# Attention of a decoder layer: projections five tiles ahead instead of four, the last tile's projection spread over two steps, and one chunk of weights split per step

## The chip, the cores and the metric

The kernel runs on one core of a Trainium2 chip. The metric is the device time of one execution in microseconds (us), as the median of several runs. The core has five engines that run their own instruction queues and wait for each other by semaphores: TensorE (PE, matrix products; its weight loads are shown as PEld), VectorE (DVE), ScalarE (ACT), GpSimd (POOL) and SyncE (SP, which issues transfers).

## The reference

One layer: differential attention over 1024 tokens and 8 heads, then a mixture of experts with 16 experts. Cut to what matters:

```python
def diff_attention(x, w_in, q_gain, k_gain, ..., subln, w_out, lambda_init):
    q, k, v = jnp.split(x @ w_in, [2 * H * dh, 4 * H * dh], axis=-1)
    q = rmsnorm(q.reshape(B, T, H, 2, dh), q_gain) * (dh ** -0.5)
    k = rmsnorm(k.reshape(B, T, H, 2, dh), k_gain)
    v = v.reshape(B, T, H, 2 * dh)
    for s in range(0, T, QBLOCK):                      # QBLOCK = 128
        e = s + QBLOCK
        sc = jnp.einsum('bqhcd,bkhcd->bhcqk', q[:, s:e], k[:, :e])
        sc = jnp.where(dist >= 0, sc - slopes * dist, -jnp.inf)
        p = jax.nn.softmax(sc, axis=-1)
        pd = p[:, :, 0] - lam * p[:, :, 1]
        outs.append(jnp.einsum('bhqk,bkhe->bqhe', pd, v[:, :e]))
    o = rmsnorm(jnp.concatenate(outs, axis=1), subln) * (1.0 - lambda_init)
    return o.reshape(B, T, H * 2 * dh) @ w_out
...
x = x + diff_attention(rmsnorm(x, norm_mix), ...)
x = x + hier_moe(rmsnorm(x, norm_ffn), ...)            # top 2 of 4 experts in the chosen group
```

## The kernel before

Attention is one loop over **steps** g. Head h and tile t of 128 queries belong to step g = 8h + t, so there are 64 of them, 0 to 63. In step g the kernel makes the scores of (h, t) and their softmax, the product with the values of step g - 1 (`pv`), and the **projection** (`qkv`) of a later tile, q = g + LEAD with LEAD = 4. The loop begins at g = -LEAD, so that LEAD projections stand ahead of the first scores. From step E0 = 60 on, where no projections are left, `out_proj` takes their place. Steps are written out in one fixed order; each engine takes its instructions in that order. The mixture of experts follows.

**A projection** has two parts of 12 products each (128 by 384). Each of the eight **chunks** c of the head's weights (128 rows) gives three: high half of x with `wH`, high half of x with `wL`, low half of x with `wH`. Part 0 takes chunks 0 to 3, part 1 chunks 4 to 7. `split_w(h, c)` makes wH on ACT (L243) and then wL on DVE (L244) from the raw chunk `wraw`, which `load_w` fetched. After part 1, ACT copies the values and the queries and keys out of PSUM (`vHL`, `qk`), squares them (`sqk`), and DVE makes the low half of the values (vHL, L323) and the sums `ssq`.

**A pair** of tiles is normalised by `qk_norm` on POOL: 14 small instructions on ssq and then the product `qn` (L339, one buffer). `qk_transpose` turns qn on PE two steps later, at the start of an odd step, and ACT and DVE write the split keys and queries (KM, AH, AL).

**Within a step** PE does: scores; in odd steps the transposes of qn; projection part 0; transposes of the previous step's softmax (`pd_transpose`); projection part 1; pv. On ACT and DVE the splits of weight chunks stand behind the softmax of the step: on DVE the order is bias and maximum (L401), KM, AL, L401 again, pdL (L426), the combination of the two softmaxes (`combine`, L410 to L412), the splits (L244), and then what follows part 1. `o_norm` (POOL, L459 to L465) scales the outputs `ou` of a finished head, and `o_transpose` (PE, L473) turns them: in step 4 of the next head, for head 6 in step 2 of head 7. In the first head each step up to the one of q = 5 also transposes the tile q + 2 of x (L274).

The order of a step around the projection:

```python
        if e >= 0:
            on1(out_proj, e, 0)
        on(qkv, q, 0)
        if t == 2 and h == H - 1:
            o_transpose(h - 1)
        on(pd_transpose, g - 1)
        on(expo, g, 1)
        on(combine, g)
        ...                    # split_w of this step
        on(qkv, q, 1)
        on(pv, g - 1)
```

Of the kernel before, what the change touches and what calls it, by code (L numbers as in the profile page):

```python
# [7 lines left out]
F32 = mybir.dt.float32  # L8
F32R = mybir.dt.float32r
BF = mybir.dt.bfloat16  # L10
# [9 lines left out]
H = 8  # L20
NT = T // 128
# [12 lines left out]
def trunk_layer_kernel(ctx, tc, a, out):  # L34
# [7 lines left out]
    def f(ap):  # L42
        return ap.bitcast(F32)
# [49 lines left out]
    def w_tile(shape, dt, name):  # L93
        return wp.tile(shape, dt, name=name, tag="w")
# [118 lines left out]
    att = es_att.enter_context(tc.tile_pool(name="att", bufs=1))  # L213
# [21 lines left out]
    def split_w(h, c):  # L235

        j = c // 3
        if c % 3 == 0:
            W["H", h, j] = w_tile([128, 3, 384], F32R, "wH")
            W["L", h, j] = w_tile([128, 3, 384], F32R, "wL")  # L240
        wh, wl, r = W["H", h, j][:, c % 3], W["L", h, j][:, c % 3], W["r", h, j][:, c % 3]
        g = gm[:, c:c + 1]
        act.activation(wh, r, AF.Copy, scale=g)  # L243
        vec.scalar_tensor_tensor(wl, r, g, f(wh), op0=OP.mult, op1=OP.subtract)  # L244
# [49 lines left out]
            other = slice(64 * (1 - c), 64 * (2 - c))  # L294
            vec.tensor_scalar(al[other, c], ident[other, None, :].to_broadcast([64, 2, 128]), 0.0, None, op0=OP.mult)
    QK, SS = {}, {}
    LEAD = 4

    def qkv(h, t, part):
        if part == 0:  # L300
            if h == 0 and t < LEAD and t % 2:
                qkv.ps = psQ.tile([128, 384], F32, name="qkv", tag="po", bufs=1)
            elif (8 * h + t >= LEAD and (t - LEAD) % NT in (0, 2)):
                qkv.ps = psS.tile([128, 384], F32, name="qkv", tag="sc")
            else:
                qkv.ps = psQ.tile([128, 384], F32, name="qkv", tag="qkv", bufs=1)
        ps = qkv.ps
        for c in range(4 * part, 4 * part + 4):
            for x, w in ((0, "H"), (0, "L"), (1, "H")):
                pe.matmul(ps, lhsT=hT[t][:, x, c], rhs=W[w, h, c // 3][:, c % 3],  # L310
                          start=(c == 0 and x == 0 and w == "H"), stop=(c == 7 and x == 1))
        if part == 1:
            rs = RX[t]
            if t % 2 == 0:
                QK[h, t // 2] = att.tile([128, 2, 4, 64], F32, name="qk", bufs=2)
                SS[h, t // 2] = att.tile([128, 2, 4], F32, name="ssq", bufs=2)
            qk = QK[h, t // 2][:, t % 2]
            v = att.tile([128, 2, 128], F32R, name="vHL", bufs=13)
            vb = att.tile([128, 128], BF, name="vb", bufs=13)
            VV[h, t] = v, vb  # L320
            act.activation(v[:, 0], ps[:, 256:], AF.Copy, scale=rs)
            act.activation(qk.rearrange("p a b -> p (a b)"), ps[:, :256], AF.Copy, scale=rs)
            vec.scalar_tensor_tensor(v[:, 1], ps[:, 256:], rs, f(v[:, 0]), op0=OP.mult, op1=OP.subtract)  # L323
            sq = att.tile([128, 4, 64], F32, name="sqk")
            act.activation(sq.rearrange("p a b -> p (a b)"), qk.rearrange("p a b -> p (a b)"), AF.Square)
            vec.tensor_reduce(SS[h, t // 2][:, t % 2], sq, axis=AX.X, op=OP.add)  # L326
            act.activation(vb, f(v[:, 0]), AF.Copy)
# [139 lines left out]
    def o_transpose(h):  # L467
        ou, sso = OU.pop(h)
        oT = att.tile([128, T], F32, name="oT")
        for g in range(2):  # L470
            ps = psQ.tile([128, 4, 128], F32, name="tp", bufs=2)
            for k in range(4):
                pe.transpose(ps[:, k], ou[g][:, k], ident)  # L473
            act.activation(oT[:, 512 * g:512 * g + 512], ps.rearrange("p a b -> p (a b)"), AF.Copy,
                           scale=sub08)
        ON[h] = oT
        if h < H - 2:
            sp.dma_start(o_dram[h], oT)
# [11 lines left out]
    def load_wout(k):  # L490

        wo["r", k] = w_tile([128, 2, 512], F32, "woraw")
        c, d = 2 * (k % 4), 512 * (k // 4)
        sp.dma_start(wo["r", k], w_out[:, c:c + 2, d:d + 512])

    def split_wout(k):
        wo[k] = big_tile([128, 2, 2, 512], F32R, "wo", k < 2)
        r = wo.pop(("r", k))
        act.activation(wo[k][:, 0], r, AF.Copy)
        (pool if k == NK - 1 else vec).tensor_sub(wo[k][:, 1], r, f(wo[k][:, 0]))  # L500
# [9 lines left out]
    def prep_o(t):  # L510
        oh = w_tile([128, H, 128], F32R, "oH")
        r = ORAW.pop(t)
        ol = w_tile([128, H, 128], F32R, "oL")
        for dst, src in ((slice(0, H - 2), r), (slice(H - 2, H - 1), ON[H - 2][:, None, t * 128:(t + 1) * 128])):
            act.activation(oh[:, dst], src, AF.Copy)
            vec.tensor_sub(ol[:, dst], src, f(oh[:, dst]))
        ot[t] = oh, ol
# [106 lines left out]
    def route(t):  # L624
        if t >= 0:
            logits(t)
            route_b(t)
        flush()
# [112 lines left out]
    def on(f_, g, *args):  # L741
        if 0 <= g < NT * H:
            f_(g // NT, g % NT, *args)

    def on1(f_, t, *args):
        if 0 <= t < NT:
            f_(t, *args)

    E0, LATE = NT * H - LEAD, 5
    def more_tokens(q):
        if q + 2 < NT:
            transpose_x(q + 2)
            for tiles in {1: [(4, 5)], 3: [(6, 7)]}.get(q, ()):
                norm_x(tiles, pool)
            if q + 5 < NT:
                load_x(q + 5)

    def crossings(g, h, t):  # L760
        if g % 2 and 0 <= g + 1 < NT * H:
            qk_transpose((g + 1) // NT, (g + 1) % NT // 2)
        if t == 4 and 0 < h < H - 1:
            o_transpose(h - 1)

    for g in range(-LEAD, E0 + LATE):
        h, t = divmod(g, NT)
        q = g + LEAD
        e = g - E0
        if t == 0 and 0 <= h < H:  # L770
            vec.tensor_scalar(bias, bias, 0.5, None, op0=OP.mult)
        on(scores, g)
        on(biased, g, 0)
        if g > 2:
            crossings(g, h, t)
        on(expo, g, 0)
        on(biased, g, 1)
        if e >= 0:
            on1(out_proj, e, 0)
        on(qkv, q, 0)  # L780
        if t == 2 and h == H - 1:
            o_transpose(h - 1)
        on(pd_transpose, g - 1)
        on(expo, g, 1)
        on(combine, g)
        if 0 <= h < H - 1:
            if h == 0:
                chunks = {0: (0, 1), 1: (2,), 2: (3, 4), 3: (5, 6, 7)}.get(t, ())
            else:
                chunks = {0: (3,), 1: (4,), 2: (5,), 3: (6, 7)}.get(t, ())  # L790
            for c in chunks:
                split_w(h + 1, c)
        if t >= 5 and 0 <= h < H - 2:
            split_w(h + 2, t - 5)
        if 0 < e + NT < NT - 1:
            c = e + NT - 1
            split_wout(c)
            if c + 4 < NK:
                load_wout(c + 4)
        if e == -1:  # L800
            prep_o(0)
        if e >= 0:
            on1(route_x, e - 1)
            on1(route_i, e - 3)
            on1(route_r, e - 2)
            on1(prep_o, e + 1)
            on1(load_o, e + 2)
            on1(load_res, e + 1)
            on1(out_proj, e, 1)
            on1(o_transpose1, e + 1)  # L810
            route(e - 1)
            on1(residual, e)
        if q == 0:
            transpose_x(1)
            norm_x((2, 3), pool)
        if g <= 2:
            crossings(g, h, t)
        on(qkv, q, 1)
        on(pv, g - 1)
        if q == 0:  # L820
            more_tokens(q)
        if q % 2 and q < NT * H:
            qk_norm(q // NT, q % NT // 2)
        if t == (1 if h < H - 1 else 0) and 0 < h < H:
            o_norm(h - 1)
        if q > 0:
            more_tokens(q)
        if g == -LEAD:
            load_params()
        if g == -LEAD + 1:  # L830
            lambda_and_gains()
            load_w(1)
        if e == -2:
            load_o(0)
        if g == 9:
            routing_constants()
        if t == 3 and 0 <= h < H - 2:
            load_w(h + 2)
        if g == E0 - NT - 1:
            load_gain()  # L840
            for c in range(4):
                load_wout(c)
        if e == -1:
            for c in (NK - 2, NK - 1):
                split_wout(c)
            o_transpose1(0)
            load_o(1)
            load_res(0)
        on1(o_norm1, g - 1 - NT * (H - 1))
# [478 lines left out]
```

## Time and profile before

| | us |
|---|---|
| median of 3 runs (1008.15 to 1012.52) | 1009.61 |
| the profiled execution: its own time | 1010.72 |
| its span, first to last instruction | 1009.0 |
| busy: PE / DVE / ACT / POOL | 940.2 / 814.7 / 753.4 / 329.5 |
| attention's steps, first scores to the end of step 59 | 33.5 to 486.1 |

The profile is one execution on the chip. Busy time is the time in which an engine had an instruction running. Idle time of an engine is written beside the instruction that ended it, with the one that it had waited for. PEclk is the share of TensorE's full clock (2.4 GHz) that was granted.

### The profile page before, as it was taken

How to read it: one execution, taken by the hardware profiler on the slowest of the kernel's cores; microseconds unless marked ns; L12 is line 12 of the kernel's file. 1: busy time of each engine (PE TensorE's matmuls, PEld its weight loads, DVE VectorE, ACT ScalarE, POOL GpSimd, SP SyncE). 2: the span in 40 equal slices, each digit the busy share in tenths (PEclk: the TensorE clock that was granted, in tenths of full speed). 3: DMA queues.
4: the chain of work that ended last, by engine and by line, in shares of the span. 5: the costliest groups of instructions: out<-in, count | busy, mean ns of one | idle time of the engine just before them, and what ended most of it. 6: DMA issues, size and time to landing. Idle time of an engine off the chain costs nothing. (4 is left out here: it accounts for less than half of the span.)

```text
span 1009.0 us, 19952 instructions
## 1 busy us (share of the span) xinstructions
PE 940.2 (93%) x7241; PEld 872.0 (86%) x7241; DVE 814.7 (81%) x1719; ACT 753.4 (75%) x1577; POOL 329.5 (33%) x977
## 2 busy tenths in 40 slices
PE   8989999999999999998899998999999999999992
PEld 7889898998988989888788886789999999999981
DVE  5788887887878888788777777999989899789880
ACT  6877777777787887877653316499899999899971
POOL 3522623325153343516764531301122212121011
PEclk9999999999999999999999999899999999999996
DMA  6320110202011020311233367789999999999923
GB/s 214 85 67 1 49 37 1 85 2 84 1 43 42 2 84 1 125 44 58 59 135 116 119 248 294 269 304 326 342 353 336 336 360 336 342 337 329 331 62 53
DMA packets 75770, 161.72 MB, mean 160 GB/s; under 512 B 8712, under 2 KB 39440, under 8 KB 67472
## 3 DMA queue, kind: packets, MB, share of 16 engines
q1 hardware_dynamic: 70544, 141.87, 39.4%
q0 software_dynamic: 5120, 18.50, 7.8%
q8 instruction: 59, 0.97, 0.4%
q14 instruction: 47, 0.39, 0.1%
HBM read 139.05 MB, written 21.30 MB: 159 GB/s over the span
## 5 line engine op out<-in xcount | busy, mean ns | idle before, releaser
L310 PE MATMUL qkv<-wH,hT 128*128 128x384 f32 x1024 | 291.3, 346 | 7.5 <-DVE vHL L323 6.2
L1005 DVE TENSOR_TENSOR mL<-raw,mH 128x2048 bf16<-128x2048 f32 x95 | 215.6, 2282 | 3.7 <-ACT mH L996 3.6
L310 PEld LDWEIGHTS qkv<-wH,hT 128*128 128x128 f32 x1024 | 188.1, 189 | 11.5 <-DVE vHL L323 9.7
L996 ACT ACTIVATE mH<-raw 128x2048 fp32r<-128x2048 f32 x95 | 177.9, 1904 | 1.2 <-POOL rs_x L56 1.2
L310 PE MATMUL qkv<-wL,hT 128*128 128x384 f32 x512 | 172.2, 336 | 0.4 <-DVE wL L244 0.4
L1071 PE MATMUL gu<-xT,mH 128*128 128x280 f32 x1024 | 156.9, 301 | 2.8 <-DVE xT L1060 1.5
L1071 PEld LDWEIGHTS gu<-xT,mH 128*128 128x128 f32 x1024 | 137.4, 190 | 3.3 <-DVE xT L1060 1.7
L1202 POOL DMA_INDIRECT out_dram<-yo,sidx x20 | 32.4, 1621 | 280.6 <-ACT yo L1200 248.5
L405 ACT ACTIVATE st<-st,nm 128x256 f32<-128x256 f32 (+7 forms) x128 | 99.2, 775 | 15.5 <-DVE nm L401 14.2
L1077 PEld LDWEIGHTS <-mL 128*128 128x128 bf16 x1536 | 93.8, 98 | 10.7
L310 PEld LDWEIGHTS qkv<-wL,hT 128*128 128x128 f32 x512 | 96.9, 189 | 0.7 <-DVE wL L244 0.7
L401 DVE CUSTOM_DVE_ANT_0 st<-sc,bias 128x256 f32<-128x256 f32 (+7 forms) x128 | 93.6, 751 | 2.2 <-PE sc L393 0.2
L426 DVE TENSOR_TENSOR pdL<-tp,pdH 128x512 bf16<-128x512 f32 (+2 forms) x96 | 50.6, 555 | 45.2 <-ACT pdH L425 45.2
L1071 PE MATMUL gu<-hx,mH 128*128 128x280 f32 x512 | 82.3, 303 | 2.4 <-DVE yT L1098 1.8
L450 ACT ACTIVATE sqo<-ou 128x128 f32<-128x128 f32 x64 | 19.9, 311 | 84.9 <-DVE ou L448 84.9
L551 PE MATMUL op<-wo,oH 128*128 128x512 f32 x256 | 81.7, 400 | 1.0 <-DVE vHL L323 0.5
L334 POOL TENSOR_SCALAR ssq<-ssq 128x8 f32<-128x8 f32 x32 | 6.3, 198 | 231.0 <-DVE ssq L326 230.9
L1077 PE MATMUL gu<-xb,mL 128*128 128x140 bf16 x1024 | 80.6, 225 | 0.0
L1071 PEld LDWEIGHTS gu<-hx,mH 128*128 128x128 f32 x512 | 68.9, 189 | 4.3 <-DVE yT L1098 3.3
L392 PE MATMUL sc<-KM,AH 128*128 128x384 f32 (+4 forms) x192 | 64.8, 344 | 0.0
L393 PE MATMUL sc<-KM,AL 128*128 128x384 f32 (+4 forms) x192 | 64.3, 341 | 0.0
L412 DVE SCALAR_TENSOR_TENSOR st<-st,sm,st 128x128 f32<-128x128 f32 (+3 forms) x64 | 61.4, 960 | 2.3
(238 smaller groups left out, 1986.1 us busy)
## 6 DMA issues: line engine op xcount, KB each, us to landing
raw<-in_moe_w_gate_dram SPq DMA_DIRECT2D x32, 1024.0 KB, 7.6
raw<-in_moe_w_up_dram SPq DMA_DIRECT2D x32, 1024.0 KB, 6.5
raw<-in_moe_w_down_dram SPq DMA_DIRECT2D x31, 1024.0 KB, 8.6
wraw<-in_da_w_in_dram SPq DMA_DIRECT2D x64, 192.0 KB, 3.3
out_dram<-xres SPq DMA_DIRECT2D x9, 512.0 KB, 5.2
xraw<-in_x_dram SPq DMA_DIRECT2D x8, 512.0 KB, 6.5
woraw<-in_da_w_out_dram SPq DMA_DIRECT2D x8, 512.0 KB, 3.8
xres<-in_x_dram SPq DMA_DIRECT2D x8, 512.0 KB, 4.3
```

Source lines behind the costliest of these rows:

```text
L310: pe.matmul(ps, lhsT=hT[t][:, x, c], rhs=W[w, h, c // 3][:, c % 3], start=(c == 0 and x == 0 and w == "H"), stop=(c == 7 and x == 1))
L392: pe.matmul(ps[:, k, :wc], lhsT=AH[h, t][:, c], rhs=KM[h][:, c, ks], start=True, stop=False)
L393: pe.matmul(ps[:, k, :wc], lhsT=AL[h, t][:, c], rhs=KM[h][:, c, ks], start=False, stop=True)
L401: vec.tensor_tensor_reduce(sv, tiles[c][:, :n, :wc], bv, -1.0, 3e38, OP.add, OP.min, nm[:, c:c + 1])
L405: act.activation(st[c][:, :w], st[c][:, :w], AF.Exp, scale=-1.0, bias=nm[:, c:c + 1], accum_out=sm[:, c:c + 1])
L412: vec.scalar_tensor_tensor(st[0][:, :w], st[1][:, :w], sm[:, 3:4], st[0][:, :w], op0=OP.mult, op1=OP.add)
L426: vec.tensor_sub(pl[:, g:g + n], ps[:, :n], f(ph[:, g:g + n]))
L551: pe.matmul(ps, lhsT=o[:, c], rhs=wo[4 * half + c // 2][:, w, c % 2], start=(c == 0 and o is oh and w == 0), stop=(c == NK - 1 and o is ol))
L996: act.activation(WH[g], full[g], AF.Copy)
L1005: vec.tensor_sub(WL[g], full[g], f(WH[g]))
L1071: pe.matmul(res[i // 2][:, i % 2, :2 * CAP], lhsT=wh[:, c - c0, 128 * i:128 * i + 128], rhs=rhs[:, c].rearrange("p a b -> p (a b)"), start ...
L1077: pe.matmul(res[i // 2][:, i % 2, :CAP], lhsT=wl[:, c - c0, 128 * i:128 * i + 128], rhs=rb[:, c], start=False, stop=(last and (c0 == 0 or ...
```

## The change

Projections run five tiles ahead (LEAD = 5), so five stand ahead of the first scores. The output projection still begins in step 60. So that the two do not leave a step empty, the projection of the last tile (63) is cut in two: part 0 in step 58, part 1 in step 59. The weights of the next head are needed a step earlier: its first projection stands in step 3 of a head instead of step 4. Chunks are split one per step (0 to 3 in steps 4 to 7 two heads ahead, 4 to 7 in steps 0 to 3 of the head before), where step 3 had two and step 4 none; `load_w` goes from step 3 to step 2. A pair's qk_norm falls into even steps; buffers of qk, ssq, vHL and vb grow by one.

```diff
-    LEAD = 4
+    LEAD = 5
...
-            elif (8 * h + t >= LEAD and (t - LEAD) % NT in (0, 2)):
+            elif 8 * h + t >= LEAD and (t - LEAD) % NT in (0, 2) and h * NT + t < NT * H - 1:
...
-                QK[h, t // 2] = att.tile([128, 2, 4, 64], F32, name="qk", bufs=2)
-                SS[h, t // 2] = att.tile([128, 2, 4], F32, name="ssq", bufs=2)
+                QK[h, t // 2] = att.tile([128, 2, 4, 64], F32, name="qk", bufs=3)
+                SS[h, t // 2] = att.tile([128, 2, 4], F32, name="ssq", bufs=3)
...
-    E0, LATE = NT * H - LEAD, 5
+    E0, LATE = NT * H - 4, 5
...
+    projections = {g: ((g + LEAD, 0), (g + LEAD, 1)) for g in range(-LEAD, E0 - 2)}
+    projections[E0 - 2] = ((NT * H - 1, 0),)
+    projections[E0 - 1] = ((NT * H - 1, 1),)
...
-        on(qkv, q, 0)
+        parts = projections.get(g, ())
+        for q, part in parts[:1]:
+            on(qkv, q, part)
...
-                chunks = {0: (0, 1), 1: (2,), 2: (3, 4), 3: (5, 6, 7)}.get(t, ())
+                chunks = {0: (0, 1), 1: (2, 3, 4), 2: (5, 6), 3: (7,)}.get(t, ())
             else:
-                chunks = {0: (3,), 1: (4,), 2: (5,), 3: (6, 7)}.get(t, ())
+                chunks = {0: (4,), 1: (5,), 2: (6,), 3: (7,)}.get(t, ())
             for c in chunks:
                 split_w(h + 1, c)
-        if t >= 5 and 0 <= h < H - 2:
-            split_w(h + 2, t - 5)
+        if t >= 4 and 0 <= h < H - 2:
+            split_w(h + 2, t - 4)
...
-        on(qkv, q, 1)
+        for q, part in parts[1:]:
+            on(qkv, q, part)
         on(pv, g - 1)
...
-        if q % 2 and q < NT * H:
+        if (NT * H - 1, 0) in parts:
+            pass
+        elif q % 2 and q < NT * H and parts:
             qk_norm(q // NT, q % NT // 2)
...
-        if t == 3 and 0 <= h < H - 2:
+        if t == 2 and 0 <= h < H - 2:
             load_w(h + 2)
```

PE in step 3 of head 2, the end of the projection's part 1 (chunks 6 and 7), with the semaphores that an instruction waits for. Before:

```order
L310 MATMUL qkv<-wH,hT 128x384 x2
L310 MATMUL qkv<-wL,hT 128x384
L310 MATMUL qkv<-wH,hT 128x384 x2
L310 MATMUL qkv<-wL,hT 128x384
L310 MATMUL qkv<-wH,hT 128x384
L437 MATMUL po<-vHL,pdH 128x256 [waits DVE_49]
```

And now:

```order
L310 MATMUL qkv<-wH,hT 128x384 [waits Activation_49]
L310 MATMUL qkv<-wL,hT 128x384
L310 MATMUL qkv<-wH,hT 128x384
L310 MATMUL qkv<-wH,hT 128x384 [waits Activation_49]
L310 MATMUL qkv<-wL,hT 128x384 [waits DVE_49]
L310 MATMUL qkv<-wH,hT 128x384
L437 MATMUL po<-vHL,pdH 128x256 [waits PE_49]
```

The products of this part are now those of the next head's first tile, and the last three wait for the wH (ACT) and the wL (DVE) of chunk 7. DVE in the same step, from the softmax's low half on, before:

```order
L426 TENSOR_TENSOR pdL<-tp,pdH 128x384
L410 RECIPROCAL sm<-sm 128x1
L411 SCALAR_TENSOR_TENSOR sm<-sm,nlam 128x1
L412 SCALAR_TENSOR_TENSOR st_2485<-st_2486,sm,st_2485 128x512
L244 SCALAR_TENSOR_TENSOR wL<-wraw_1778,gm,wH 128x384 x2
L323 SCALAR_TENSOR_TENSOR vHL<-qkv,rs_x_558,vHL 128x128
```

And now:

```order
L426 TENSOR_TENSOR pdL<-tp,pdH 128x384
L410 RECIPROCAL sm<-sm 128x1
L411 SCALAR_TENSOR_TENSOR sm<-sm,nlam 128x1
L412 SCALAR_TENSOR_TENSOR st_2551<-st_2552,sm,st_2551 128x512
L244 SCALAR_TENSOR_TENSOR wL<-wraw_1726,gm,wH 128x384
L323 SCALAR_TENSOR_TENSOR vHL<-qkv,rs_x_198,vHL 128x128
```

One of two splits has left the step; the one that stays, chunk 7, stands behind the combination of step 3. POOL at the start of head 7, where head 6 is normalised (epso, rs_o, ou are o_norm's), before:

```order
L57 TENSOR_SCALAR rs_o<-rs_o 128x8
L58 TENSOR_TENSOR rs_o<-rs_o 128x8
L465 TENSOR_TENSOR ou<-ou,rs_o 128x512 x2
L334 TENSOR_SCALAR ssq<-ssq 128x8
L52 TENSOR_SCALAR rs_qk<-ssq 128x8
L54 TENSOR_TENSOR rs_qk<-rs_qk 128x8
```

And now:

```order
L57 TENSOR_SCALAR rs_qk<-rs_qk 128x8
L58 TENSOR_TENSOR rs_qk<-rs_qk 128x8
L339 TENSOR_TENSOR qn<-qk,rs_qk 128x512
L459 TENSOR_TENSOR epso<-sm 128x8
L460 TENSOR_SCALAR epso<-epso 128x8
L461 TENSOR_SCALAR epso<-sso 128x8
```

The pair that was normalised behind o_norm (its ssq at L334 follows ou) now stands ahead of it: o_norm of head 6 begins behind one more qk_norm.

## Rows read from the trace of the kernel before

**Rows 1.** Stretches: us, busy time of each engine (instructions), granted clock, DMA.

```profile
20.00:30.00 10.00, 10.00 (x65) 9.65 (x63) 6.30 (x18) 7.84 (x20) 6.62 (x30) 1.00 0.45 124
155.40:215.00 59.60, 56.82 (x374) 53.67 (x374) 48.52 (x118) 46.67 (x128) 22.27 (x79) 1.00 0.12 37
```

**Rows 2.** Waits of PE in head 2, 155.4 to 215: us, times, longest.

```profile
PE tp L352 <- POOL qn L339: 1.3, 2, 0.7
PE tp L424 <- DVE AL L369: 0.7, 2, 0.5
PE qkv L310 <- DVE vHL L323: 0.7, 1, 0.7
```

**Rows 3.** Timeline of PE, steps 3 and 4 of head 2: start, us, instruction.

```profile
180.58 0.33 PE L310 MATMUL qkv<-wL,hT 128*128 128x384 f32 x1
...
181.73 0.31 PE L392 MATMUL sc<-KM,AH 128*128 128x320 f32 x1
```

**Rows 4.** Timeline of ACT, step 3 of head 2.

```profile
175.96 0.31 ACT L450 ACTIVATE sqo<-ou 128x128 f32<-128x128 f32 x1 [0.69 <-DVE ou L448]
...
180.99 1.11 ACT L243 ACTIVATE wH<-wraw,gm 128x384 fp32r<-128x384 f32 x2
```

**Rows 5.** Timeline of DVE, step 3 of head 0 and of head 2.

```profile
62.36 0.75 DVE L412 SCALAR_TENSOR_TENSOR st<-st,sm,st 128x512 f32<-128x512 f32 x1
...
181.78 1.50 DVE L412 SCALAR_TENSOR_TENSOR st<-st,sm,st 128x512 f32<-128x512 f32 x1
183.20 1.13 DVE L244 SCALAR_TENSOR_TENSOR wL<-wraw,gm,wH 128x384 fp32r<-128x384 f32 x2
```

**Rows 6.** Timeline of POOL, step 3 of head 2.

```profile
180.69 2.04 POOL L465 TENSOR_TENSOR ou<-ou,rs_o 128x512 f32<-128x512 f32 x2
```

**Rows 7.** Timeline of PE, projections of tiles 2 and 3 at the start.

```profile
22.46 0.42 PE L310 MATMUL qkv<-wH,hT 128*128 128x384 f32 x1
...
27.50 0.42 PE L310 MATMUL qkv<-wH,hT 128*128 128x384 f32 x1
```

**Rows 8.** Waits of PE in steps 0 to 3 of head 0.

```profile
PE tp L274 <- issue: 1.3, 1, 1.3
PE tp L352 <- DVE hT L279: 0.5, 1, 0.5
```

**Rows 9.** Timeline of DVE, end of step 0 of head 7.

```profile
463.21 0.40 DVE L326 TENSOR_REDUCE ssq<-sqk 128x4 f32<-128x256 f32 x1
```

**Rows 10.** Timeline of POOL, steps 0 to 3 of head 7.

```profile
463.88 0.20 POOL L459 TENSOR_TENSOR epso<-sm 128x8 f32<-128x8 f32 x1
...
468.77 2.04 POOL L465 TENSOR_TENSOR ou<-ou,rs_o 128x512 f32<-128x512 f32 x2
472.90 0.20 POOL L334 TENSOR_SCALAR ssq<-ssq 128x8 f32<-128x8 f32 x1 [2.09 <-DVE ssq L326]
...
476.87 1.05 POOL L339 TENSOR_TENSOR qn<-qk,rs_qk 128x512 f32<-128x512 f32 x1
```

**Rows 11.** Timeline of PE, step 2 of head 7.

```profile
471.80 1.04 PE L473 MATMUL tp<-ident,ou 128*128 128x128 f32 x8
```

**Rows 12.** Waits of PE, steps 0 to 3 of head 7 (columns as in Rows 2).

```profile
PE po L437 <- DVE pdL L426: 2.8, 2, 2.2
PE tp L352 <- POOL qn L339: 1.7, 1, 1.7
```

**Rows 13.** Timeline of SP, step 3 of head 2.

```profile
178.17 7.40 SPq L232 DMA_DIRECT2D wraw<-in_da_w_in_dram  x8
```

**Rows 14.** Stretches around waits of PE (columns as in Rows 1).

```profile
6.70:9.20 2.50, 0.88 (x3) 0.63 (x4) 2.31 (x5) 2.50 (x6) 0.00 (x0) 1.00 1.00 284
9.30:12.60 3.30, 2.92 (x10) 2.41 (x8) 3.21 (x6) 2.82 (x6) 0.00 (x0) 0.50 0.87 283
...
483.20:485.40 2.20, 0.05 (x1) 0.05 (x1) 1.54 (x4) 2.15 (x7) 1.73 (x7) 1.00 0.00 0
485.40:488.00 2.60, 2.08 (x15) 1.78 (x15) 2.49 (x7) 2.18 (x7) 2.10 (x7) 1.00 0.00 0
```

More of the change, by code (lines that the diff above doesn't have):

```diff
@@ L314, in qkv @@
             if t % 2 == 0:
-                QK[h, t // 2] = att.tile([128, 2, 4, 64], F32, name="qk", bufs=2)
-                SS[h, t // 2] = att.tile([128, 2, 4], F32, name="ssq", bufs=2)
+                QK[h, t // 2] = att.tile([128, 2, 4, 64], F32, name="qk", bufs=3)
+                SS[h, t // 2] = att.tile([128, 2, 4], F32, name="ssq", bufs=3)
             qk = QK[h, t // 2][:, t % 2]
-            v = att.tile([128, 2, 128], F32R, name="vHL", bufs=13)
-            vb = att.tile([128, 128], BF, name="vb", bufs=13)
+            v = att.tile([128, 2, 128], F32R, name="vHL", bufs=14)
+            vb = att.tile([128, 128], BF, name="vb", bufs=14)
             VV[h, t] = v, vb
```

## The prediction

> **What bounds the kernel now.** I began with the table of stretches, which gives busy time per engine in a piece of the span. In head 2, which stands for all the middle heads, a head takes 59.60 us and PE is busy for 56.82 of them, DVE for 53.67, ACT for 48.52, all at full clock [rows 1]. PE sets the pace, with about 2.8 us per head left to win. The view of waits says where they lie: 1.3 us for qn (two waits), 0.7 for the low half of the values (vHL), 0.7 for AL (two waits) [rows 2]; the sum is 2.7. So a gain is bounded by these waits, and any new wait of PE costs in full. DVE and ACT have only 6 and 11 us of slack per head, and inside a step they run as one chain behind the scores. The question is therefore: which product of PE now waits for something that comes late in that chain?
>
> I then read the timelines of step 3 of head 2, engine by engine. PE does the wL product of chunk 7 at 180.58, and step 4 starts at 181.73 [rows 3]. ACT starts sqo at 175.96 and works without a gap until the two wH at 180.99 [rows 4]. DVE begins its combination at 181.78, needs 1.50 us for it, and makes wL of chunks 6 and 7 from 183.20, 0.57 us each [rows 5]. Before the change nobody waits for these splits: they serve the next head, one step later.
>
> **The change: the start.** One more projection step stands ahead of the first scores. Projections there are 5.04 us apart (22.46 to 27.50) [rows 7], and PE is busy for all 10.00 of the 10 us from 20 to 30 [rows 1], so nothing hides it: +5.0. The steps behind lose nothing by it, as the same work is taken out of steps 58 and 59, whose account comes below. Some comes back in head 0: PE waits there 1.3 us in issue and 0.5 for hT [rows 8], which belong to the transposes of x and now have an earlier tile's lead. I take −1.8; the bounds are −0.6 (only hT) and −2.4 (another small wait too). Start: +3.2.
>
> **The chunk-7 wait.** With projections five ahead, step 3 of heads 0 to 6 projects the first tile of the next head. Its part 1 needs chunk 7, and chunk 7 is split in that same step, on DVE behind the combination. PE reaches this product earlier than before: the step-1 wait for qn (0.6) and the step-3 wait (0.7) [rows 2] go, since qk_norm now stands a step earlier. The first passes on only in part, about 0.5, because pv still needs pdL. So PE comes at 180.58 − 1.2 = 179.4. DVE's chain moves only with the scores, by 0.5: the combination begins at 181.3. It took 1.50 us beside the two ou products of POOL, which ran at 180.69 for 2.04 [rows 5, 6]; the same operation took 0.75 in head 0 [rows 5]. POOL's o_norm comes a step earlier now, so I take 0.75: it ends at 182.0, and the one wL that is left at 182.6. With 0.1 to 0.2 less for the small operation ahead of it, the wait is **3.1 us**. If the combination stays at 1.50, it is 3.9; if the whole 1.3 us reaches the scores, 2.3. These are the bounds.
>
> What goes in exchange: all of the old waits, 2.7. qn is ready earlier; vHL and AL are made by ACT and DVE, and PE comes to them later by the new wait's size, while one more split (0.57 on DVE) in step 4 takes some of that lead. Net per head 3.1 − 2.7 = +0.4, with bounds of −0.4 and +1.2; I take +0.3, as head 0's old waits are longer. Seven heads: **+2** (−3 to +8).
>
> **Head 7.** On POOL qk_norm of pair 2 now stands ahead of o_norm of head 6. Its last ssq comes with tile 61, now projected in step 0; DVE finishes such a sum at 463.6 [rows 9]. A qk_norm takes 5.0 us (472.90 to 476.87 plus 1.05), o_norm 6.9 (463.88 to 468.77 plus 2.04) [rows 10]. So ou is ready at about 475.6 instead of 470.8. On PE the transposes of ou in step 2 ran at 471.80 without waiting [rows 11]; everything behind them on PE (pd_transpose, pv, step 59) now waits until 475.6, 3.8 us. The wait of 1.7 for qn goes, and part of those 2.8 us for pdL [rows 12]. Projection work of 5 us leaves steps 58 and 59, but from 483.20 to 485.40 PE did 0.05 us of work while ACT was busy 2.15 of 2.20 [rows 14]: softmax, not PE, ends these steps, so it gives little back. I take **+2**, from +1 to +4.
>
> **At nothing:** load_w moves from step 3 to step 2 on SP. Its issue takes 7.40 us of SP [rows 13], and the last two of its chunks wait for the raw buffer until chunk 7 is split; behind it stands only the store of oT of step 4, for which nobody on PE waits. If that cover were gone, it would delay o_dram alone. The bigger buffers remove waits only. Part 1 of tile 63 stands ahead of pd in step 59, so its copies come before pdH on ACT: inside the +1 to +4.
>
> Sum without the clock: 3.2 + 2 + 2 = 7.2.
>
> **The clock.** Before, PE runs at full clock nearly everywhere. But after it had been busy for only 0.88 of 2.50 us at 6.7, the next 3.30 us were granted 0.50; after the wait of 2.2 us at 483.20 the clock stayed full [rows 14]. Half of 2.4 GHz is the lower of the two levels. My wait of 3.1 us is longer than both. In a stretch of 3.3 us at half clock PE loses up to 1.65 us; a part of that falls on times in which it waits anyway or on slack, so I take 0.9 for each of the seven waits: **+6** (0 to +11).
>
> The Trainium skill, "TensorE: Matmul & The Clock Gate", Part 1: The HAM clock gate, says that activity is what releases the throttle and that idle returns the engine to its slow state. By that rule the change is bad beyond the bare wait; by the row of 2.2 us alone the clock term would be 0 and the total 1016.8.
>
> Total: 1010.7 (the profiled execution) + 7.2 + 6 = 1023.9; medians stand 1.1 us lower: **1023**.
>
> **The rivals.**
> *B, the wait without the clock:* the same waits of about 3 us, the clock stays full, as after 483.20 [rows 14]. 1009.6 + 7.2 = 1017, from 1012 to 1019. Against it: that wait is the shorter one, and there are seven chances.
> *C, faster:* the chunk-7 wait is short, because the ACT and DVE chains of step 3 follow PE closer than I think (all 1.3 us and the quicker combination, less work ahead). At 1.5 us a head gains 1.2 net, seven heads 8.4, the clock stays full: 1009.6 + 3.2 + 2 − 8.4 = 1006; at 1.0 it is 1003. It decides at a wait of about 2.0 us: below it the seven heads pay for start and head 7. Against it: DVE's chain begins with scores that PE makes in the same step, and ACT had no gap in it from 175.96 on [rows 4].
> *D, no net change:* wait near 2.2, start returns 2.4, head 7 costs 1: 1009.6 + 2.6 + 1 − 3 = 1010, from 1006 to 1013.
>
> **How the numbers follow.** A change below about 0.5% (5 us) can't be told from none in this kernel. Forecast (about 3 us of wait with clock loss, 1018 to 1030): 0.50. B: 0.25. D: 0.15. C: 0.10. The range reaches down to the middle of D and up to the sum of the upper bounds of head and clock taken in half: 1009 to 1031. It leaves out C and a little above. C lies about half under 1004.6, D half of its upper part; faster 0.08, same 0.20 (D, the rest of C, the low end of B), slower 0.72.
>
> **What the changed profile would show.** First scores near 38.5 instead of 33.5. In step 3 of heads 0 to 6, a wait of PE at L310 for DVE wL, 2.3 to 3.9 us, seven times, and none for qn; the waits for vHL and AL gone or under 0.3. In head 7 a wait at L473 for POOL ou of 4 to 5.5 us. Granted clock 0.50 in a stretch behind most of the seven waits. Wrong if PE waits there under 2 us, if the old waits stay beside the new one (then above 1031), or if steps 58 and 59 become shorter by more than 3 us.

## The result, and the profile after

The changed kernel takes 1033.90 us (median of 4 runs, 1029.81 to 1036.05), the kernel before 1009.58 beside it: a ratio of 1.0225, 95% interval 1.0201 to 1.0249, so 2.3% slower. The forecast was slower, 1023 us, with a range of 1009 to 1031: right in sign, too small, and outside the range.

The profiled execution is the fastest of the four (1029.81, span 1028.1), 19.1 us more than the profiled one of before (span 1009.0). Where they lie is read from PE's timeline, at the first scores of a head. In the changed kernel these are the first scores of all, of heads 1, 2, 3 and 7, and of step 60:

```profile
39.94 0.31 PE L392 MATMUL sc<-KM,AH 128*128 128x128 f32 x1
...
103.02 0.22 PE L392 MATMUL sc<-KM,AH 128*128 128x128 f32 x1
...
164.61 0.22 PE L392 MATMUL sc<-KM,AH 128*128 128x128 f32 x1
...
226.32 0.22 PE L392 MATMUL sc<-KM,AH 128*128 128x128 f32 x1
...
473.80 0.22 PE L392 MATMUL sc<-KM,AH 128*128 128x128 f32 x1
...
508.45 0.39 PE L392 MATMUL sc<-KM,AH 128*128 128x320 f32 x1
```

In the kernel before, the same rows stand at 33.47, 95.30 (head 1), 454.58 (head 7) and 486.08 (step 60). The differences:

| stretch | before | after | measured | predicted |
|---|---|---|---|---|
| up to the first scores | 33.5 | 39.9 | +6.5 | +5.0 |
| head 0 | 61.8 | 63.1 | +1.2 | −0.6 (−1.8 start, +0.3 wait, +0.9 clock) |
| heads 1 to 6 | 359.3 | 370.8 | +11.5 | +7.2 (six times 0.3 + 0.9) |
| head 7 up to step 60 | 31.5 | 34.7 | +3.2 | +2 |
| the rest | 522.9 | 519.6 | −3.3 | 0 |

Head 2 and its step 3, in the view of stretches of the changed kernel (columns as in [rows 1]): the head, the wait, the 3.4 us behind it, then head 7 up to step 60 and a part of it.

```profile
164.60:226.30 61.70, 58.37 (x374) 55.34 (x373) 47.30 (x118) 46.66 (x127) 21.67 (x79) 0.97 0.12 35
188.40:191.90 3.50, 0.69 (x2) 0.43 (x3) 2.46 (x7) 1.73 (x5) 1.62 (x4) 1.00 0.01 2
192.20:195.60 3.40, 3.40 (x17) 3.26 (x16) 2.04 (x6) 1.75 (x6) 0.00 (x0) 0.50 0.44 123
489.20:502.70 13.50, 10.90 (x37) 9.12 (x38) 6.06 (x17) 6.03 (x17) 10.75 (x37) 0.50 0.00 0
473.80:508.50 34.70, 27.59 (x149) 24.70 (x148) 23.21 (x59) 23.54 (x65) 19.89 (x74) 0.80 0.14 42
```

The same 374 instructions of PE as in [rows 1] are busy for 58.37 us instead of 56.82, and PE idles for 3.3 instead of 2.8. The extra busy time is the clock: PE is nearly idle for 3.5 us, then busy without a gap for 3.40 at 0.50. The waits of PE in this head:

```profile
PE qkv L310 <- ACT wH L243: 1.8, 1, 1.8
PE qkv L310 <- DVE wL L244: 1.0, 1, 1.0
PE tp L424 <- DVE AL L369: 0.5, 2, 0.3
```

Against [rows 2], qn and vHL are gone, AL has shrunk from 0.7 to 0.5, and 2.8 us for chunk 7 have come. The timeline of step 3, ACT, DVE and PE in order of time, shows why:

```profile
189.56 0.60 ACT L243 ACTIVATE wH<-wraw,gm 128x384 fp32r<-128x384 f32 x1
...
190.21 0.44 PE L310 MATMUL qkv<-wH,hT 128*128 128x384 f32 x1 [1.83 <-ACT wH L243]
190.32 0.75 DVE L412 SCALAR_TENSOR_TENSOR st<-st,sm,st 128x512 f32<-128x512 f32 x1
190.99 0.61 DVE L244 SCALAR_TENSOR_TENSOR wL<-wraw,gm,wH 128x384 fp32r<-128x384 f32 x1
...
191.65 0.44 PE L310 MATMUL qkv<-wL,hT 128*128 128x384 f32 x1 [1.00 <-DVE wL L244]
```

The combination takes 0.75, as in head 0 before [rows 5], since POOL's ou no longer runs beside it. Already wH of chunk 7 is late for PE, and wL, behind the combination, once more.

Ahead of the first scores PE waits in two places that the forecast had as gone, and in head 7 in four (views of waits, 33 to 40 us and 473.8 to 508.5):

```profile
PE tp L274 <- issue: 1.4, 1, 1.4
PE tp L274 <- DVE AL L369: 0.5, 1, 0.5
```

```profile
PE po L437 <- DVE pdL L426: 3.8, 2, 2.7
PE qkv L310 <- DVE vHL L323: 1.4, 1, 1.4
PE po L441 <- DVE pdL L426: 1.2, 1, 1.2
PE tp L473 <- POOL ou L465: 0.7, 1, 0.7
```

### The profile page after: what moved, and what is told of

It is laid out like the page before. It is cut to its first block, busy times and chain, and to the rows that moved or that the text cites. A ratio compares the mean times of both kernels' runs of the same rounds, so it can differ in the third digit from the quotient of the medians.

```text
span 1028.1 us, 19950 instructions
## 1 busy us (share of the span) xinstructions
PE 951.5 (93%) x7241; PEld 884.6 (86%) x7241; DVE 801.7 (78%) x1719; ACT 754.2 (73%) x1577; POOL 324.7 (32%) x977
## 5 line engine op out<-in xcount | busy, mean ns | idle before, releaser
L310 PE MATMUL qkv<-wH,hT 128*128 128x384 f32 x1024 | 295.5, 350 | 16.0 <-ACT wH L243 14.1
L310 PEld LDWEIGHTS qkv<-wH,hT 128*128 128x128 f32 x1024 | 190.4, 191 | 20.8 <-ACT wH L243 16.5
L310 PE MATMUL qkv<-wL,hT 128*128 128x384 f32 x512 | 174.8, 341 | 7.1 <-DVE wL L244 7.1
L1087 PEld LDWEIGHTS <-mL 128*128 128x128 bf16 x1536 | 93.8, 98 | 10.7
L426 DVE TENSOR_TENSOR pdL<-tp,pdH 128x512 bf16<-128x512 f32 (+2 forms) x96 | 50.6, 555 | 61.6 <-ACT pdH L425 61.5
L334 POOL TENSOR_SCALAR ssq<-ssq 128x8 f32<-128x8 f32 x32 | 6.3, 197 | 253.8 <-DVE ssq L326 253.2
L392 PE MATMUL sc<-KM,AH 128*128 128x384 f32 (+4 forms) x192 | 68.7, 362 | 2.8 <-DVE KM L367 2.8
L393 PE MATMUL sc<-KM,AL 128*128 128x384 f32 (+4 forms) x192 | 68.1, 360 | 0.5 <-DVE AL L369 0.5
L551 PEld LDWEIGHTS op<-wo,oH 128*128 128x128 f32 x256 | 46.9, 188 | 9.6 <-DVE xres L554 0.6
```

The lines of the kernel that those rows point to most:

```text
L392: pe.matmul(ps[:, k, :wc], lhsT=AH[h, t][:, c], rhs=KM[h][:, c, ks], start=True, stop=False)
L393: pe.matmul(ps[:, k, :wc], lhsT=AL[h, t][:, c], rhs=KM[h][:, c, ks], start=False, stop=True)
L426: vec.tensor_sub(pl[:, g:g + n], ps[:, :n], f(ph[:, g:g + n]))
L551: pe.matmul(ps, lhsT=o[:, c], rhs=wo[4 * half + c // 2][:, w, c % 2], start=(c == 0 and o is oh and w == 0), stop=(c == NK - 1 and o is ol))
L1087: pe.matmul(res[i // 2][:, i % 2, :CAP], lhsT=wl[:, c - c0, 128 * i:128 * i + 128], rhs=rb[:, c], start=False, stop=(last and (c0 == 0 or ...
```

## The experiments

Ratios are to the kernel before, timed on the same chip, with 95% intervals. The changed kernel itself has 1.0225 and, on another chip, 1.0271 (below).

**Chunk 7 a step earlier.**

```diff
-chunks = {0: (0, 1), 1: (2, 3, 4), 2: (5, 6), 3: (7,)}   # head 0
+chunks = {0: (0, 1), 1: (2, 3, 4), 2: (5, 6, 7)}
-chunks = {0: (4,), 1: (5,), 2: (6,), 3: (7,)}
+chunks = {0: (4,), 1: (5,), 2: (6, 7)}
```

> The changed kernel with chunk 7 split in step 2 of a head instead of step 3 (chunks 6 and 7 together there), all else the same. Theory A (the late chunk 7 sets the loss): the 2.8 us wait of PE in step 3 and the half clock behind it are both gone in heads 1 to 6, a head takes 57.5 to 58.5 us instead of 61.7, first scores stay near 39.9, total 1004 to 1012. Rival R1 (ACT and DVE are simply too late for projections one tile further ahead, whichever product asks first): the wait moves to the next thing that they make (vHL, AL, pdL), a head stays at 61 or more, total above 1025. Rival R2 (the clock falls for another reason than this wait): the wait goes but the stretches at 0.50 remain, a head takes about 59.5, total 1015 to 1020.

Measured: 1014.13 us, ratio 1.0049 (1.0032 to 1.0065). Head 2 in the view of stretches, and its waits:

```profile
164.60:223.30 58.70, 56.60 (x374) 53.88 (x373) 47.38 (x118) 46.45 (x127) 21.99 (x79) 1.00 0.12 37
```

```profile
PE po L437 <- DVE pdL L426: 1.6, 1, 1.6
PE tp L424 <- DVE AL L369: 0.5, 2, 0.3
```

Full clock, no wait for a split, and a head 3.0 us shorter than in the changed kernel, 0.9 shorter than before the change. So theory A holds, but not whole: 1.6 us of the 2.8 come back at the next thing that the chain makes late, pdL for pv, which is the mechanism of R1. The total is above the forecast's 1012; the first scores, which the forecast had near 39.9, stand at 43.5 in this profile.

**A smaller dose: chunk 7 earlier within step 3.**

```diff
+        if t == 3 and 0 <= h < H - 1:
+            split_w(h + 1, 7)
         on(expo, g, 1)
         on(combine, g)
...                               # 3: (7,) taken out of both tables
```

> The changed kernel with the split of chunk 7 kept in step 3, but put ahead of the second exponential (ACT) and of the combination (DVE). A smaller dose of the same wait: wH about 0.7 us earlier, wL about 1.4 earlier, so PE waits 1.3 to 1.6 us instead of 2.8. Theory A with the clock as a threshold-like effect of the wait: the clock stays full in steps 3 and 4, a head takes 58.5 to 59.8, total 1012 to 1018. If the clock falls at this shorter wait as well: a head takes about 60.3, total 1020 to 1024. If the later combination costs as much as the earlier split saves: 61 or more, total as the changed kernel.

Measured: 1020.74 us, ratio 1.0115 (1.0096 to 1.0135). The waits of head 2, then stretches: head 2, head 3, and 3.4 us behind the wait in head 2 and in head 3.

```profile
PE qkv L310 <- ACT wH L243: 1.1, 1, 1.1
PE qkv L310 <- DVE wL L244: 0.8, 1, 0.8
```

```profile
164.20:223.50 59.30, 56.89 (x374) 53.92 (x374) 47.49 (x118) 46.59 (x128) 21.68 (x79) 1.00 0.12 37
223.50:284.30 60.80, 58.38 (x374) 55.37 (x373) 47.52 (x118) 46.65 (x127) 21.68 (x79) 0.97 0.12 36
190.00:193.40 3.40, 3.08 (x25) 3.04 (x25) 2.81 (x8) 1.71 (x7) 0.00 (x0) 1.00 0.40 114
250.50:253.90 3.40, 3.40 (x17) 3.36 (x15) 2.76 (x8) 1.50 (x6) 0.00 (x0) 0.50 0.42 121
```

The wait is 1.9 us in heads 2 to 6, more than expected, and 1.4 in heads 0 and 1, where no fall of the clock followed. The same wait of 1.9 was followed by half clock in heads 3, 5 and 6 and not in 2 and 4. Two heads of one run with the same work and the same waits differ by 1.5 us: that is the price of one fall of the clock. Theory A's "threshold" is no sharp one.

**The wait kept, PE kept busy.**

```diff
             for i, (x, w) in enumerate(((0, "H"), (0, "L"), (1, "H"))):
+                for _ in range((10, 5, 0)[i] if fill is not None else 0):   # chunk 7 of tile 0
+                    pe.matmul(fill[...], lhsT=hT[t][:, 0, 6], rhs=W["H", h, 2][:, 0], ...)
                 pe.matmul(ps, lhsT=hT[t][:, x, c], rhs=W[w, h, c // 3][:, c % 3], ...)
```

> The changed kernel with 15 products more in step 3 of heads 0 to 6, written to a PSUM tile that nobody reads: ten of 0.17 us ahead of chunk 7's wH product, five ahead of its wL product, so that PE is busy while it waits; the results are the same. It tells the clock from the wait. If idle PE is what halves the clock: the stretches at 0.50 behind step 3 go, PE's busy share fills the 2.8 us, and a head takes 60.2 to 60.7 us instead of 61.7, total 7 to 11 lower than the changed kernel. If the clock falls for another reason: 0.50 stays, a head 61.7 or more, total the same or higher by up to 3.

Measured: 1024.96 us, ratio 1.0169 (1.0152 to 1.0186), against 1035.58 for the changed kernel on the same chip: 10.6 less, at the end of the expected 7 to 11. Head 2 in stretches, and the end of its step 3 on PE (L312 are the added products, L314 the projection):

```profile
162.90:223.10 60.20, 59.45 (x389) 56.42 (x389) 47.13 (x118) 46.63 (x128) 21.68 (x79) 1.00 0.12 36
```

```profile
186.51 1.90 PE L312 MATMUL tp<-wH,hT 128*128 128x384 f32 x10
188.52 0.44 PE L314 MATMUL qkv<-wH,hT 128*128 128x384 f32 x1
188.80 1.04 PE L312 MATMUL tp<-wH,hT 128*128 128x384 f32 x5
189.96 0.44 PE L314 MATMUL qkv<-wL,hT 128*128 128x384 f32 x1
```

PE does 15 products more and the head is 1.5 us shorter, at full clock. Chunk 7 comes no earlier by this, so the wait and the clock are told apart: at full clock the change costs 0.6 us per head (60.2 against 59.6 [rows 1]); the clock adds 1.5. In the profiles the gain lies in heads 1 to 6, 361.9 us instead of 370.8. Head 0 gains nothing (63.0 against 63.1): its one stretch at half clock stands behind another wait, that of step 2 (below), in both.

**Both kernels once more.** Unchanged sources.

> The changed kernel once more, for a second profile: the first one was the fastest of its four runs (1029.8, median 1033.9). If the spread comes from the start (PE waits there for x from DRAM, and the clock falls): first scores move from 39.9 to between 39 and 44, heads 1 to 6 stay at 61.7, and the total follows the start. If it comes from the heads: the number of stretches at half clock there differs from one per head.

> The kernel before once more, one look, for the spread of its start: first scores at 33.5 in its first profile, with one stretch at half clock. If the start spreads by itself, 33 to 37 here, heads 59.6 as before; otherwise 33.5.

Measured: the changed kernel 1035.58 us, ratio 1.0271 (1.0254 to 1.0288); its profiled execution, 1041.69, was the slowest of five. First scores stood at 45.7, outside what was expected, and head 0 took 68.7 instead of 63.1; heads 2, 3 and 5 took 61.7 again, head 1 60.0 (no fall of the clock behind its wait), head 4 63.1. The start in stretches:

```profile
10.00:14.00 4.00, 2.04 (x8) 1.47 (x6) 2.86 (x6) 2.91 (x6) 0.00 (x0) 0.54 0.99 386
14.00:18.00 4.00, 3.36 (x13) 3.36 (x14) 0.23 (x1) 2.50 (x5) 1.54 (x8) 0.50 0.58 229
18.00:22.00 4.00, 4.00 (x21) 3.90 (x21) 1.64 (x4) 3.23 (x9) 2.69 (x14) 0.68 0.15 38
```

PE waits there for x from DRAM, and the clock is at half for some 10 us. The kernel before took 1007.66 in its one run, first scores at 32.4. In the 12 profiles with five projections ahead and nothing added at the start, the first scores stand between 39.2 and 45.7, median 41.8; in the three with four, the control below among them, at 32.4 to 33.5. The first case holds in part: of the 11.9 us between the two profiles of the changed kernel 5.7 are the start and 5.6 head 0, while heads 1 to 6 took 371.0 and 370.8 together. The spread of the starts goes with the clock. Between 6 and 22 us the granted clock was 1.00 in three of the 12 profiles (first scores at 39.2 to 39.9), 0.89 in one (39.6), 0.79 in six (41.8 to 43.0) and 0.68 in two (43.5 and 45.7); with four projections ahead it was 0.89 in all three.

**Head 0: fewer splits in step 1.** In the changed kernel the scores of step 2 wait for KM, which on DVE stands behind three wL:

```profile
51.05 2.46 DVE L244 SCALAR_TENSOR_TENSOR wL<-wraw,gm,wH 128x384 fp32r<-128x384 f32 x3
53.53 0.87 DVE L367 TENSOR_TENSOR KM<-tp,KM 64x256 fp32r<-64x256 f32 x2
...
54.10 0.41 PE L392 MATMUL sc<-KM,AH 128*128 128x384 f32 x1 [2.78 <-DVE KM L367]
```

```diff
-chunks = {0: (0, 1), 1: (2, 3, 4), 2: (5, 6), 3: (7,)}
+chunks = {0: (0, 1, 2), 1: (3,), 2: (4, 5, 6), 3: (7,)}
```

> The changed kernel with the splits of head 0 moved: chunks 0, 1, 2 in step 0, chunk 3 alone in step 1 (three there now), 4, 5, 6 in step 2, chunk 7 still in step 3. If the three splits, which stand ahead of KM and AL in step 1, make the 3.2 us wait of the scores of step 2: that wait falls to about 1, and the stretch at half clock at 55.65 goes as well; total 3 lower than the changed kernel. Rival (start-up waits for the first keys in any case): the same 3.2 us, perhaps at another instruction, total unchanged within 1 us.

Measured: 1030.32 us, ratio 1.0217 (1.0198 to 1.0237). The wait fell to 1.5 us, but head 0 took 63.0 as against 63.1: steps 1 and 2 became 2.9 shorter, steps 3 and 4 longer by as much, since PE now waited 2.9 for chunk 7 and the half clock moved there. The mechanism was right, its gain went to the next wait.

**Head 7.** Three runs: o_norm of head 6 ahead of qk_norm on GpSimd; tile 63 whole in step 58; and products that nobody reads (written as in step 3) in the waits.

```diff
+        if t == 0 and h == H - 1:
+            o_norm(h - 1)                  # first run: ahead of qk_norm
...
-    projections[E0 - 2] = ((NT * H - 1, 0),)
-    projections[E0 - 1] = ((NT * H - 1, 1),)
+    # second run: both parts in step E0 - 2
...
+        if g == 58: filler(8, ...)         # third run; ahead of part 0
+        if t == 2 and h == H - 1: filler(8, ...)     # ahead of o_transpose
+        if 57 <= g <= 59: filler((6, 6, 14)[g - 57], ...)   # ahead of pv
```

> The changed kernel with o_norm of head 6 put ahead of the qk_norm of pair 2 on GpSimd, as it stood before. If the late ou is what costs in head 7: the wait at L473 (0.7) goes, ou is ready 5 us earlier, head 7 to the end of step 59 takes 32.5 instead of 34.7 us, total 2 lower than the changed kernel. Rival: PE arrives at L473 late anyway, since it waits for vHL first and runs at half clock there; then nothing moves by more than 0.7 us.

> The changed kernel with the projection of tile 63 whole in step 58 and none in step 59 (the spread undone). If the cut of tile 63 costs in head 7 (its part 0 waits for vHL and runs at half clock in step 58, its part 1's copies stand ahead of pdH in step 59): step 59 shortens from 9.0 to about 7.5 us, and the total is 1 to 2 lower than the changed kernel. Rival (the steps end by the softmax chain, whatever PE projects): steps 58 and 59 together stay within 1 us of 20.8, total unchanged. Third: one fuller and one empty step make a longer idle PE in step 59, 2 or more slower.

> The kernel with products in the step 3 waits, and in head 7 more of them, again written to a tile that nobody reads: 8 ahead of part 0 of tile 63 and 8 ahead of the transposes of ou in step 58, 6, 6 and 14 ahead of the pv of steps 57, 58 and 59. If idle PE and the clock set head 7's loss: the long stretch at half clock there (10 to 14 us) goes or shrinks to one, steps 56 to 59 take 31 to 33 us instead of 34.7, step 60 about 14.2, total 3 to 4 lower than with the step 3 products alone (1025). Rival (softmax and GpSimd set these steps): clock full, steps 56 to 59 still 34 or more, total 1024 to 1027.

The order alone: 1035.33 us, ratio 1.0254 (1.0230 to 1.0278), steps 56 to 59 35.2: no gain, the wait for ou went and the one for vHL doubled. Tile 63 whole: 1035.22, ratio 1.0260 (1.0241 to 1.0279), steps 58 and 59 21.1 us against 20.8: no gain either, the rival's "unchanged". Their waits, first the order, then tile 63:

```profile
PE po L437 <- DVE pdL L426: 5.8, 2, 4.4
PE qkv L310 <- DVE vHL L323: 2.9, 1, 2.9
```

```profile
PE po L437 <- DVE pdL L426: 4.4, 1, 4.4
PE qkv L310 <- DVE vHL L323: 1.4, 1, 1.4
...
PE tp L473 <- POOL ou L465: 0.7, 1, 0.7
```

In both the clock was at half in step 58. With the products: 1020.55 us, ratio 1.0113 (1.0091 to 1.0134), 4.4 below those of step 3 alone (each against the kernel before, about 1008.7); of this the two profiles show 1.5 in head 7 (35.4 and 33.9 us). The clock was full in head 7, yet steps 56 to 59 took 34.0; PE now came early enough to wait for ou (L477 here):

```profile
465.50:499.50 34.00, 30.34 (x192) 27.79 (x190) 23.10 (x59) 23.46 (x65) 19.41 (x71) 1.00 0.14 43
```

```profile
PE tp L477 <- POOL ou L469: 1.5, 2, 1.1
```

So the order was tried again with the clock full, and, as eight products then stood where no wait was left, once more without these eight. With the old order these eight cost nothing, since PE still waited for ou behind them; that kernel without the eight was not run.

```diff
         if t == 2 and h == H - 1:
-            filler(8, 7, 7, 6)
             o_transpose(h - 1)
```

> The kernel with the products in step 3 and in head 7, and o_norm of head 6 ahead of the qk_norm of pair 2 on GpSimd. With the clock full, PE waited there 1.4 us for ou behind 1.4 us of products. If ou's place sets the rest of head 7: those waits go, step 58 takes 8 to 9.5 us instead of 10.95, steps 56 to 59 take 32 to 33 instead of 34.0, total 1 to 2 lower (1019). Rival: as in the run with the order alone, DVE's vHL comes later beside the product of ou, PE waits there instead, steps 56 to 59 stay at 33.5 or more.

> The kernel with products in step 3 and head 7 and with o_norm first, less the 8 products ahead of the transposes of ou, which had no wait left to fill. If they alone hid the gain of the order: step 58 takes 9.3 instead of 10.7 us, steps 56 to 59 32.3 instead of 33.7, total 1 to 1.5 lower. Rival (the chain through vHL, the last projection and the softmax sets the step): step 58 at 10.2 or more, 33.3 or more in all.

Measured: 1020.17 us (ratio 1.0105, 1.0082 to 1.0128), steps 56 to 59 33.7, as the rival had it; without the eight, 1019.63 (1.0105, 1.0090 to 1.0121), step 58 9.3 and all four steps 32.3, as the first case said to a tenth.

```profile
466.60:498.90 32.30, 28.70 (x183) 26.44 (x182) 24.58 (x59) 23.34 (x65) 17.48 (x63) 1.00 0.14 45
```

The two causes hide each other: at half clock PE is late, and an early ou helps nobody; at full clock PE waits for ou. Together they make 2.4 of the 3.2 us. In the total, taking the eight out shows as no more than 0.5 us, inside the spread.

**Can the change be made to pay?** Both waits for splits taken away by order; then products at the start and in head 7 added; then o_norm first; then the eight products out. The control is the kernel before with the start's products.

```diff
+chunks = {0: (0, 1, 2), 1: (3, 4), 2: (5, 6, 7)}       # head 0; {0: (4,), 1: (5,), 2: (6, 7)} later
...
         if q == 0:
+            filler(8, 0, 0, 0)
             transpose_x(1)
```

> The changed kernel with both waits for splits taken away by order alone: chunk 7 in step 2 in all heads, and in head 0 chunks 0, 1, 2 in step 0, 3, 4 in step 1, 5, 6, 7 in step 2. Heads 1 to 6 58.7 us, as with chunk 7 in step 2 alone; head 0 61 to 62 instead of 63.1; total 1008 to 1013, so still not below the kernel before, because the start (first scores at 39 to 44) and head 7 (34.7) keep what the heads give. If the start were the smaller part: 1003 to 1006.

> The same with products that nobody reads in the places where PE idles long: 8 at the start ahead of the transposes of the second tile, and those of head 7. If the clock in the first 20 us is what makes the start spread: first scores at 39 to 40 in most runs, a narrower spread, head 7 31 to 33, total 1001 to 1006, below the kernel before. If the fillers only push work back: total as the kernel without them, 1008 to 1013.

> The splits moved, the products at the start and in head 7, and o_norm of head 6 first. If ou's place sets the rest of head 7: 1 to 2 lower than 1011, so within 0.2 per cent of the kernel before on either side. Rival: 1010 to 1012, unchanged.

> The variant with the splits moved, the products at the start and in head 7, and o_norm first, less the same 8 products. If they hid the gain: 1009.5 to 1010.5, within 0.15 per cent of the kernel before. Rival: 1011 to 1012.

> The kernel before with the same 8 products at the start: the control for the start. Its first scores are at 32.4 to 33.5 with one stretch at half clock near 9.3. If the products keep the clock up there: 31.5 to 32.5, total 0 to 2 lower; if they only push: 1 higher.

Measured, in this order: 1014.29 us, ratio 1.0045 (1.0028 to 1.0063); 1010.96, 1.0019 (1.0005 to 1.0033); 1011.79, 1.0023 (1.0011 to 1.0034); 1009.58, 1.0017 (1.0005 to 1.0028); the control 1008.62, 0.9999 (0.9988 to 1.0009). None beats the kernel before; the first two are above what was expected of them (1013 and 1006 at most), the fourth came as expected. The start has no more gain in it for the kernel before (first scores at 33.2, one stretch at half clock still there); with five projections they stood at 40.6, 40.0 and 39.3 in the three profiles with the products, the low end of those without, at a granted clock of 1.00 between 6 and 22 us. In the profile of the fourth, heads 1 to 6 take 352.1 us instead of 359.3, head 0 61.3 instead of 61.8 and head 7 32.3 instead of 31.5; the start, 5.8 to 6.9 longer, takes nearly all of it.

## Why the prediction was wrong, by its own steps

**The chunk-7 wait: right.** It stands in step 3 of each of heads 0 to 6, 2.65 us in heads 0 and 1 and 2.8 to 2.9 in the others, against 3.1 forecast. It begins at wH, which ACT makes behind the second exponential (I had read its time and not counted it as a wait), and ends at wL. The waits for qn and vHL went as forecast; those for AL did not (0.5 us stay). At full clock the price is 0.6 per head (the run with products) instead of 0.3: within its bounds.

**The clock: the mechanism right, the term mis-sized.** I took 0.9 us for each wait, "a part of that falls on times in which it waits anyway or on slack". It falls on neither: PE is busy for 3.40 of 3.40 us at 0.50. A fall costs 1.5, shown by two heads of one run and by the 8.9 us that the products gave back in heads 1 to 6; and head 1, with its wait but no fall, took 60.0 in the second profile, as with the products, against 61.6 in the first. The bound of 1.65 was the better value. In the first profile six of the seven waits had a fall behind them; head 0 had one too, but behind the wait of step 2. The Trainium skill, "TensorE: Matmul & The Clock Gate", Part 1: The HAM clock gate, says that activity releases the throttle and that an idle engine goes back to its slow state; the falls behind the waits agree. Here products of no use kept the clock full as well.

**The start: the step that failed, in sign.** The −1.8 that should come back in head 0 was reasoned from an earlier tile's lead. The wait for hT went; the wait in issue, and one of 0.4 for AL behind it, did not: they stand ahead of the first scores now (1.4 + 0.5). The times in the traces show what they wait for. The transposes of x and those of qn in the same step use the same two buffers of tp. The first four transposes of x begin when DVE's KM ends (it ended at 46.80 and they began at 46.89 before the change, 38.30 and 38.40 now), the other four when AL ends. Before, this was tile 7 in step 1; now it is tile 6 in the last projection step, where ACT comes to KM late, behind the square of a tile of x (sqx) for which it waited for DRAM:

```profile
35.60 1.06 ACT L258 ACTIVATE sqx<-xraw 128x1024 f32<-128x1024 f32 x1 [0.94 <-DMA xraw<-in_x_dram]
36.66 0.75 ACT L363 ACTIVATE KM<-tp 64x256 fp32r<-64x256 f32 x2
37.44 0.86 DVE L367 TENSOR_TENSOR KM<-tp,KM 64x256 fp32r<-64x256 f32 x2 [2.99 <-ACT KM L363]
38.40 0.63 PE L274 MATMUL tp<-ident,xraw 128*128 128x128 f32 x4 [1.36 <-issue]
```

So the start is 5.04 + 1.9 − 0.7 (the second tile's transposes began 0.7 earlier in that execution, 12.93 against 13.62) = +6.2, and measured +6.5. Two things in head 0 the forecast did not have at all: a new wait of 3.2 for KM and AL, behind three splits, with the fall of the clock behind it; and one tile's transposes of x, 1.0 us of PE, which went ahead of the first scores too.

**Head 7: near by luck, for another reason.** +3.2 against +2 (+1 to +4). The wait at the transposes of ou was to be 4 to 5.5 us and was 0.7: PE came late, held by vHL and 13.5 us at half clock. The order on GpSimd that I blamed counts only once the clock is full. Of the 3.2, 0.8 stay with both causes away; what they are wasn't tried.

**The rest.** The profiled execution flatters the change. Its 3.3 us less behind step 60 are spread, not gain: that stretch took 519.4 to 523.2 us in the other profiles here, 520.5 in the second one of the kernel before. And its start is among the shortest. With the median of the starts, 41.8, in place of 39.9, the table gives 8.3 to 9.4 + 1.2 + 11.5 + 3.2 = 24.2 to 25.3, and the medians differ by 24.3. So of the missing 11 us 5 to 6 are the start with the −1.8 that did not come back, some 4 the clock and the bare wait in heads 1 to 6, 1 head 7. Either of the first two alone would have left the time inside the range; together they did not. Of the start, 1.9 us (41.8 against 39.9) go with the clock in the first 22 us. Why that clock fell more often with five projections than with four isn't settled: the first 15 us hold the same work, and three profiles of the shorter start are few.

## What to carry to other kernels

When a product is moved ahead, check each of its operands for where it is made in the new step, and price a new wait of a nearly always busy TensorE as the wait plus the clock that it takes away: here half a wait more. A wait at a certain instruction may belong to a buffer that others in the same step hold: find out what frees it before you count the wait as gone. Two causes in one stretch can hide each other, so an undone part that changes nothing isn't yet acquitted.

## What the runs showed of the hardware

- The granted clock fell behind waits as short as 1.9 us (1.1 + 0.8, three heads of five), and stayed full behind others of the same length in the same run, behind the 2.65 us in head 0 of the first profile of the changed kernel and behind the 2.65 us in head 1 of the second: in these runs a wait of 2 to 3 us was a chance of a fall, not a certainty.
- Products into a PSUM tile that nobody reads kept the clock full where a wait was there to fill: 15 of them made a head 1.5 us shorter. They cost nothing there: head 1 took 60.0 us with them and 60.0 without them in the profile where its clock did not fall. Where no wait was, eight cost 1.4 us (step 58, 10.7 against 9.3).
- DVE's combination of 128x512 took 1.50 us beside POOL's product of ou [rows 5, 6], six times of six in the kernel before, and 0.75 the other two times; in the changed kernel, where ou runs in the step before, all eight took 0.75.
